# Contracting over all 128 rows: low key parts stored twice, compressed values zero-padded per head

## The chip, the cores and the metric

One core of one Trainium2 chip runs the kernel; the other cores are idle. The metric is the device time of one execution in microseconds (us), taken as the median of several runs.

## The reference, cut to what matters

Two decoder layers, sequence length 512, model width 1024, all in float32. Each layer normalises x, makes one wide projection, runs three token mixers on it (sparse attention, differential attention, a spatial gating MLP), merges them by gates, and ends with a SwiGLU FFN. The change touches the two attention mixers.

```python
# sparse attention (8 heads of 64 in 2 groups, query block of 128 rows)
logit_c = einsum('btghd,bngd->bghtn', qg, kc) * scale     # 31 compressed keys
p_c = masked_softmax(logit_c, ...)
o_cmp = einsum('bghtn,bngd->btghd', p_c, vc)              # compressed values
logit_s = einsum('btghd,bgtkd->bghtk', qrg, ks) * scale   # selected blocks, rotated keys
logit_w = einsum('btghd,bkgd->bghtk', qrg, kw) * scale    # window, rotated keys
out = g0 * o_cmp + g1 * o_slc + g2 * o_win
# differential attention (4 heads, two maps each, depth 64)
logits = einsum('bthd,bshd->bhts', q, k) * scale
a = p[:, :, 0] - lam * p[:, :, 1]
o = einsum('bhts,bshe->bthe', a, v)
```

Selected-block and window attention over 512 positions both come out as plain causal attention here, so the kernel has for each sparse head two causal maps ("kind" 0 and 1), and for each differential head two more.

## The kernel before, in words

To keep float32 accuracy with the fast float32r matmul, every operand is split into a high part (rounded) and a low part (the rest); a product takes three matmuls in the big GEMMs (high by high, low weight by high, high weight by low: lines 164 to 166). ScalarE makes the high part of each 128x1024 weight chunk (L144), VectorE or GpSimd the low part (L147), two chunks ahead of use; SyncE issues the weight loads (L125) four chunks ahead, with three raw buffers.

The work of a layer is a list of GEMM tasks. Two side lanes hold the attention work; after every GEMM step (three matmuls of 512 columns, counted as 650 ns) the side lanes are advanced by as many of their own steps as the count allows. So matmuls of attention lie between matmuls of GEMMs in TensorE's order, which is fixed when the program is built. Each `yield` in a lane is one such step.

Heads of depth 64 are stored so that rows 0 to 63 and 64 to 127 of a query tile hold the high and the low part. `rope_pair` rotates the four heads of a task, splits them, writes the parts to DRAM (L600) and reads them back in the layout wanted: the high part of the keys twice, on rows 0 to 63 and again on 64 to 127 (`kh`, L611); the low part of the keys once per head, two heads over each other in one tile `kl` (L614); the queries (`q2`) as high over low, or low over high for the heads that stand in the lower half of `kl` (L623, L626). `logits` (L778) then makes one block of 128 query rows in two matmuls: L783 over 128 rows gives (high + low) query by high key; L784 over 64 rows gives high query by low key. The block has 128, 256, 384 or 512 columns. `soft` subtracts the maximum (L773, VectorE) and takes the exponential (L775, ScalarE); `nsa` scales by sum and gate (L808 VectorE, L809 GpSimd), transposes by TensorE (L826), splits (L827 ScalarE, L833 VectorE) and multiplies by the values (L847); units follow each other at a distance of three (`LAG`). `diff` does the same with lines 917 to 949.

The compressed branch: `cmp_aux("v")` makes the compressed values of both groups, the same 32 rows four times over (`VCS`, L556 to L559: high in columns 0 to 63, low in 64 to 127). Its probabilities stand as `PcT`, 32 rows for each of four heads. For a head, L854 contracts over that head's 32 rows, twice (high and low part of the probabilities), into the accumulator `o` of L847.

Tiles come from pools: "t4" (36 buffers of 4 KB per row), "t2" (12 of 2 KB); logits have two PSUM banks ("s"), transposes two ("t"), accumulators one ("o"), GEMMs three ("g").

Of the kernel before, what the change touches and what calls it, by code (L numbers as in the profile page):

```python
# [11 lines left out]
F32 = mybir.dt.float32  # L12
# [15 lines left out]
# Emission distances: how many steps after its cause each part of a chain is traced.  # L28
D_FIN = (10, 17, 31, 34)        # norm of a differential head
D_CMP = (0, 5, 8, 12, 15, 26)   # softmax over compressed blocks  # L30
D_ROPE = (2, 11, 16, 19)        # split, store and reload of rotated heads
D_MX, D_ACT, D_OA, D_XP = (25, 27), (7, 19), (1, 4, 17), 2
D_NORM = (10, 13)              # must lie before the first evacuation of its group
W_NSA, W_DIFF, LAG = 500, 1300, 3
POOLED = {"w": 512, "u": 512, "g": 512}   # low-part columns made by GpSimd, by task
# [11 lines left out]
def chunk_table():  # L47
    """Name of each weight chunk of a layer -> (index, columns used)."""
# [27 lines left out]
class Kern:  # L76
# [12 lines left out]
    # ---------------------------------------------------------------- tiles  # L89
# [16 lines left out]
    # ----------------------------------------------------- delayed emission  # L106
# [13 lines left out]
    # -------------------------------------------------------------- weights  # L120
# [38 lines left out]
    # ----------------------------------------------------------- GEMM tasks  # L159
# [8 lines left out]
    def fm(self, i0, evacs, x, K=KT, late=False, hooks=None):  # L168
        """Feature-major products of len(evacs) weight chunks with the tiles x."""
# [20 lines left out]
    def tm(self, i0, x, evac, kper, n):  # L190
        """Token-major products: four token tiles, n columns."""
# [18 lines left out]
    # ------------------------------------------------------------- constants  # L210
# [44 lines left out]
    def pin(self, first, mark):  # L255
        """Instructions from first to mark stay in trace order on their engines, later ones behind them."""
# [18 lines left out]
    def setup2(self):  # L275
        """Differential lambda, halved merge bias, scaled sub-norm, rotary tables."""
# [99 lines left out]
    # ------------------------------------------------------------ RMS norms  # L376
    def make_xg(self, k, gcol, fast=None):
        """Gain-scaled high and low parts of x, and its squares."""
# [23 lines left out]
    def square0(self, k):  # L402
        """Squares of the first layer's input: two running sums, on two engines."""
# [40 lines left out]
    # --------------------------------------------------------- evacuations  # L444
# [66 lines left out]
    def cmp_aux(self, which):  # L511
# [32 lines left out]
        else:  # L544
# [15 lines left out]
            yield 1300  # L560

    def rope_pair(self, name, raw=None):
        """Evacuates the first- and second-half tiles of four heads, rotates and splits them."""
        st = {}

        def fa(ps):
# [930 lines left out]
```

## Time and profile before

| | us |
|---|---|
| median of 3 runs | 1886.5 |
| lowest, highest | 1885.8, 1887.4 |
| span of the profiled execution, first to last instruction | 1884.8 |
| TensorE busy in it | 1851.9 |
| VectorE busy in it | 1021.5 |
| ScalarE busy in it | 734.3 |
| GpSimd busy in it | 409.3 |

The three runs lie within 1.6 us. The span of the profiled execution is 1.7 us below the median. PE is TensorE's matmuls, PEld its weight loads, which may run beside matmuls; the end of a matmul in the trace is modelled, its start is not, so this text reads TensorE by the distance from one start to the next.

### The profile page before, as it was taken

To read this page: it belongs to the slowest core of one execution; us is meant where nothing else is said; L and a number is where in the kernel's file an instruction comes from. 1 tells how busy PE (TensorE), PEld (TensorE's weight loads), DVE (VectorE), ACT (ScalarE), POOL (GpSimd) and SP (SyncE) were. 2 spreads that over 40 slices of the span, in tenths; PEclk is the share of its full clock that TensorE was granted. 3 is DMA by queue.
4 is the path that set the end of the run, shared out by engine and by line. 5 is a ranking of instruction groups with operands and counts; after the bars stand their busy time and mean duration, and the time that the engine had idled before them with its cause. 6 is when DMAs were issued, how large, how long until landed. Compare 5 with 4: busy or idle time off the path is not lost.

```text
span 1884.8 us, 23458 instructions
## 1 busy us (share of the span) xinstructions
PE 1851.9 (98%) x8686; PEld 1493.7 (79%) x8686; DVE 1021.5 (54%) x1928; ACT 734.3 (39%) x1300; POOL 409.3 (22%) x391
## 2 busy tenths in 40 slices
PE   6999999999999999999999999999999999999997
PEld 5787777777888888888878877787778888888887
DVE  8657665557554444443355766656665544444323
ACT  4446554344333223222233555534443433223222
POOL 3324331234321000000042333313333200000001
PEclk9999999999999999999999999999999999999999
DMA  5542112543232222223346221154422322222221
GB/s 194 170 154 90 40 46 92 183 138 117 87 112 89 101 99 92 101 94 119 112 140 207 88 79 40 51 163 132 133 104 101 106 95 96 101 94 96 101 95 62
DMA packets 70787, 203.22 MB, mean 108 GB/s; under 512 B 9360, under 2 KB 11792, under 8 KB 70672
## 3 DMA queue, kind: packets, MB, share of 16 engines
q1 hardware_dynamic: 70672, 201.71, 32.1%
q8 instruction: 69, 1.13, 0.2%
q14 instruction: 46, 0.38, 0.1%
HBM read 182.67 MB, written 19.01 MB: 107 GB/s over the span
## 4 chain that ended last, share of the span: by engine, by line
PE 95%; DVE 2%; issue 2%; POOL 1%; DMA 0%; ACT 0%; DVEq 0%; SPq 0%; POOLq 0%
PE ps_g L164 26%; PE ps_g L165 25%; PE ps_g L166 25%; PE ps_s L784 3%; PE ps_o L847 2%; PE ps_t L826 2%; PE ps_s L783 2%; PE ps_g L203 1%; PE ps_g L202 1%; PE ps_g L201 1%; PE ps_o L945 1%; PE ps_o L854 1%; DVE wl L147 1%; POOL wl L147 1%; PE ps_o L203 0%
## 5 line engine op out<-in xcount | busy, mean ns | idle before, releaser
L164 PE MATMUL ps_g<-xg,wh 128*128 128x512 f32 x1408 | 573.6, 407 | 9.1 <-ACT wh L144 8.4
L144 ACT ACTIVATE wh<-wr 128x1024 fp32r<-128x1024 f32 (+2 forms) x324 | 318.2, 985 | 668.4 <-PE ps_g L166 369.2
L165 PE MATMUL ps_g<-xg,wl 128*128 128x512 f32 x1408 | 555.0, 394 | 7.0 <-DVE wl L147 7.0
L166 PE MATMUL ps_g<-xg,wh 128*128 128x512 f32 x1408 | 553.8, 393 | 0.0
L147 DVE TENSOR_TENSOR wl<-wr,wh 128x1024 fp32r<-128x1024 f32 (+2 forms) x312 | 358.1, 1149 | 227.2 <-ACT wh L144 226.0
L164 PEld LDWEIGHTS ps_g<-xg,wh 128*128 128x128 f32 x1408 | 266.7, 189 | 79.7 <-issue 12.5
L165 PEld LDWEIGHTS ps_g<-xg,wl 128*128 128x128 f32 x1408 | 266.9, 190 | 57.4 <-DVE wl L147 8.9
L166 PEld LDWEIGHTS ps_g<-xg,wh 128*128 128x128 f32 x1408 | 266.5, 189 | 56.4 <-issue 0.4
L775 ACT ACTIVATE e<-e,nm 128x128 f32<-128x128 f32 (+1 forms) x192 | 107.4, 559 | 137.3 <-DVE nm L773 134.3
L164 PE MATMUL ps_g<-act,wh 128*128 128x512 f32 (+1 forms) x374 | 141.0, 377 | 0.0
L165 PE MATMUL ps_g<-act,wl 128*128 128x512 f32 (+1 forms) x374 | 140.8, 376 | 0.0
L166 PE MATMUL ps_g<-act,wh 128*128 128x512 f32 (+1 forms) x374 | 140.8, 376 | 0.0
L147 POOL TENSOR_TENSOR wl<-wr,wh 128x512 fp32r<-128x512 f32 x72 | 112.2, 1563 | 83.0 <-ACT wh L144 77.6
L809 POOL TENSOR_SCALAR e<-e,sm,ga 128x128 f32<-128x128 f32 (+3 forms) x128 | 85.1, 666 | 180.3 <-DVE sm L808 167.4
L773 DVE CUSTOM_DVE_ANT_0 e<-ps_s,con 128x128 f32<-128x128 f32 (+1 forms) x192 | 93.1, 485 | 50.6 <-PE ps_s L784 48.9
L400 POOL TENSOR_TENSOR acc<-acc,sq 128x512 f32<-128x512 f32 x18 | 29.1, 1616 | 387.6 <-ACT sq L399 387.6
L1086 DVE TENSOR_TENSOR fb<-ps_g,R 128x512 f32<-128x512 f32 x44 | 30.4, 692 | 129.1 <-PE ps_g L166 129.1
L1077 DVE TENSOR_TENSOR fa<-ps_g,R 128x512 f32<-128x512 f32 x44 | 30.4, 692 | 95.6 <-PE ps_g L166 95.6
L166 PEld LDWEIGHTS ps_g<-act,wh 128*128 128x128 f32 x374 | 70.4, 188 | 13.0
L164 PEld LDWEIGHTS ps_g<-act,wh 128*128 128x128 f32 x374 | 70.4, 188 | 12.9
L165 PEld LDWEIGHTS ps_g<-act,wl 128*128 128x128 f32 x374 | 70.4, 188 | 12.8
L833 DVE TENSOR_TENSOR pt<-ps_t,pt 128x128 fp32r<-128x128 f32 (+3 forms) x128 | 61.9, 487 | 31.4 <-ACT pt L827 29.9
(229 smaller groups left out, 2589.0 us busy)
## 6 DMA issues: line engine op xcount, KB each, us to landing
wr<-in_wst SPq DMA_DIRECT2D x268, 512.0 KB, 3.2
rp_d<-pc SPq DMA_DIRECT2D x112, 128.0 KB, 2.6
wr<-in_wst SPq DMA_DIRECT2D x48, 256.0 KB, 2.7
kh<-rp_d SPq DMA_DIRECT2D x24, 256.0 KB, 4.3
xT<-in_xT SPq DMA_DIRECT2D x8, 512.0 KB, 5.6
q<-rp_d SPq DMA_DIRECT2D x16, 256.0 KB, 4.1
q<-rp_d SPq DMA_DIRECT2D x32, 128.0 KB, 3.5
kl<-rp_d SPq DMA_DIRECT2D x12, 256.0 KB, 6.2
```

Of the source, the lines that this page charges most:

```text
L144: nc.scalar.activation(h[:, a:b], t[:, a:b], AF.Copy)
L147: eng.tensor_tensor(lo[:, a:b], t[:, a:b], h[:, a:b].bitcast(F32), op=OP.subtract)
L164: nc.tensor.matmul(out, wh[:, c], xx[:, 0, ts], start=first, stop=False)
L165: nc.tensor.matmul(out, wl[:, c], xx[:, 0, ts], start=False, stop=False)
L166: nc.tensor.matmul(out, wh[:, c], xx[:, 1, ts], start=False, stop=last)
L773: nc.vector.tensor_tensor_reduce(out=e[:, :n], in0=s[:, :n], in1=self.mask[:, S - n:], scale=-0.125, scalar=3e38, op0=OP.add, op1=OP.min, ...
L775: nc.scalar.activation(e[:, :n], e[:, :n], AF.Exp, bias=nm, scale=-1.0, accum_out=sm)
L783: nc.tensor.matmul(s[:, :n], q[:, ts], k[:, :n], start=True, stop=False)
L784: nc.tensor.matmul(s[:, :n], q[r0:r0 + 64, ts], kl[r0:r0 + 64, :n], start=False, stop=True)
L809: nc.gpsimd.tensor_scalar(e[:, :n], e[:, :n], sm, gate, op0=OP.mult, op1=OP.mult)
L826: nc.tensor.transpose(pt[:, j, :], e[:, j * P:(j + 1) * P], self.ident)
L833: nc.vector.tensor_tensor(lo, pt, hi.bitcast(F32), op=OP.subtract)
```

## The change

The low parts of the keys are stored like the high parts: twice, on rows 0 to 63 and 64 to 127, in two tiles instead of one, loaded by four transfers instead of two. All query tiles are now high over low, one transfer of 128 rows per head. The second matmul of `logits` contracts over all 128 rows, (high + low) query by low key. The compressed values get a copy for each of the four heads, zero outside that head's 32 rows (four multiplications by columns of the block mask), and L854's matmul contracts over all 128 rows. `VCS` moves from a buffer of its own into the "t4" pool, and `cmp_aux("v")` has one more step. The other lines of the diff drop comments.

```diff
             for g in range(2):
                 for k in range(2):
                     nc.tensor.matmul(pv[:, g, :], hT[:, k, g].rearrange("p r n -> p (r n)"),
                                      w2[:, 512 + k * 64:512 + k * 64 + 64], start=(k == 0), stop=(k == 1))
-            self.VCS = self.const("VCS", [P, 2, P], F32R)
-            nc.scalar.activation(self.VCS[:, :, 0:64], pv, AF.Copy)
-            nc.vector.tensor_tensor(self.VCS[:, :, 64:128], pv, self.VCS[:, :, 0:64].bitcast(F32),
-                                    op=OP.subtract)
+            vcs = self.t2("vcs", (P, 2, P), F32R)
+            nc.scalar.activation(vcs[:, :, 0:64], pv, AF.Copy)
+            nc.vector.tensor_tensor(vcs[:, :, 64:128], pv, vcs[:, :, 0:64].bitcast(F32), op=OP.subtract)
             yield 1300
+            self.VCS = self.t4("VCS", [P, 4, 2, P], F32R)
+            for h in range(4):
+                col = C_BLK + 32 * h
+                nc.vector.tensor_scalar(self.VCS[:, h], vcs.bitcast(F32), self.con[:, col:col + 1], None,
+                                        op0=OP.mult)
+            yield 1300
...
                     kh = [self.t4("kh", [P, 2, S], F32R) for _ in range(2)]
-                    kl = self.t4("kl", [P, 2, S], F32R)
+                    kl = [self.t4("kl", [P, 2, S], F32R) for _ in range(2)]
                     for c in range(2):
-                        for r in range(2):
-                            nc.sync.dma_start(kh[c][64 * r:64 * r + 64].bitcast(F32),
-                                              d[0:64, 2 * c:2 * c + 2, :])
-                    for r in range(2):
-                        nc.sync.dma_start(kl[64 * r:64 * r + 64].bitcast(F32), d[64:128, r::2, :])
+                        for x, k in enumerate((kh, kl)):
+                            for r in range(2):
+                                nc.sync.dma_start(k[c][64 * r:64 * r + 64].bitcast(F32),
+                                                  d[64 * x:64 * x + 64, 2 * c:2 * c + 2, :])
                     self.rot[name] = (kh, kl)
                 else:
                     q = [self.t4("q2", [P, 2, S], F32R) for _ in range(2)]
                     for c in range(2):
                         for j in range(2):
                             h = 2 * c + j
-                            if (name == "QA1") or (name[1] == "B" and j == 1):
-                                for r in range(2):
-                                    nc.sync.dma_start(q[c][64 * r:64 * r + 64, j, :].bitcast(F32),
-                                                      d[64 - 64 * r:128 - 64 * r, h, :])
-                            else:
-                                nc.sync.dma_start(q[c][:, j, :].bitcast(F32), d[:, h, :])
+                            nc.sync.dma_start(q[c][:, j, :].bitcast(F32), d[:, h, :])
...
-    def logits(self, q, k, kl, r0, i):
+    def logits(self, q, k, kl, i):
+
         nc = self.nc
         n = (i + 1) * P
         ts = slice(i * P, (i + 1) * P)
         s = self.bank("s")
         nc.tensor.matmul(s[:, :n], q[:, ts], k[:, :n], start=True, stop=False)
-        nc.tensor.matmul(s[:, :n], q[r0:r0 + 64, ts], kl[r0:r0 + 64, :n], start=False, stop=True)
+        nc.tensor.matmul(s[:, :n], q[:, ts], kl[:, :n], start=False, stop=True)
         return s
...
-            s = self.logits(q2[hh // 2][:, hh % 2], kh[kind][:, g], kl[:, kind], 64 * g, i)
+            s = self.logits(q2[hh // 2][:, hh % 2], kh[kind][:, g], kl[kind][:, g], i)
...
-                rows = slice(32 * hh, 32 * hh + 32)
                 for x in range(2):
-                    nc.tensor.matmul(o, self.VCS[rows, g, :],
-                                     self.PcT[g][rows, x, half * 256:half * 256 + 256],
+                    nc.tensor.matmul(o, self.VCS[:, hh, g, :],
+                                     self.PcT[g][:, x, half * 256:half * 256 + 256],
                                      start=False, stop=(x == 1))
...
-            s = self.logits(q2[c][:, j], kh[c][:, j], kl[:, c], 64 * j, i)
+            s = self.logits(q2[c][:, j], kh[c][:, j], kl[c][:, j], i)
```

## Rows read from the trace of the kernel before

**Rows 1.** The page: the span, busy time of TensorE and VectorE (share of the span, instructions), and the chain of work that ended last, by engine.

```profile
span 1884.8 us, 23458 instructions
PE 1851.9 (98%) x8686; PEld 1493.7 (79%) x8686; DVE 1021.5 (54%) x1928; ACT 734.3 (39%) x1300; POOL 409.3 (22%) x391
...
PE 95%; DVE 2%; issue 2%; POOL 1%; DMA 0%; ACT 0%; DVEq 0%; SPq 0%; POOLq 0%
```

**Rows 2.** Busy time of each engine in stretches of the span (start:end in us, length, then busy us and instructions of each engine, granted TensorE clock, busy share of the DMA engines, GB/s): two stretches of the first layer's sparse attention, one of its differential attention, and the first stretch of the second layer's sparse attention.

```profile
130.00:165.00 35.00, 35.00 (x184) 26.50 (x183) 30.85 (x103) 25.15 (x76) 18.36 (x25) 1.00 0.21 64
165.00:200.00 35.00, 34.99 (x179) 25.82 (x178) 22.24 (x67) 19.44 (x51) 12.17 (x17) 1.00 0.23 73
370.00:410.00 40.00, 40.00 (x187) 30.83 (x187) 24.24 (x64) 16.95 (x38) 13.93 (x12) 1.00 0.63 170
1055.00:1090.00 35.00, 35.00 (x181) 26.42 (x181) 31.08 (x104) 25.01 (x77) 18.65 (x24) 1.00 0.20 65
```

**Rows 3.** Groups of TensorE instructions with their shapes kept apart: rows x columns of the weights and of the streamed operand, how many, busy us, mean ns of one. L784 comes in four widths, 48 of each; the widest and the narrowest are shown.

```profile
L784 PE MATMUL ps_s<-kl,q 64*128 64x512 f32 x48 | 23.8, 496 | 0.0
...
L854 PE MATMUL ps_o<-pcT,VCS 32*128 32x256 f32 x64 | 15.9, 327 | 0.0
L784 PE MATMUL ps_s<-kl,q 64*128 64x128 f32 x48 | 15.5, 324 | 0.0
```

**Rows 4.** The weight loads of L784 in the same view: count, busy us, mean ns, then the idle time of the weight loader just before them and what it was put down to.

```profile
L784 PEld LDWEIGHTS ps_s<-kl,q 64*128 64x128 f32 x192 | 35.1, 183 | 49.0 <-issue 47.0
```

**Rows 5.** TensorE's instructions in order of time around one logits block of 512 columns (start us, duration us): first the matmuls, then three of the weight loads.

```profile
230.87 0.40 PE L783 MATMUL ps_s<-kh,q 128*128 128x512 f32 x1
231.20 0.50 PE L784 MATMUL ps_s<-kl,q 64*128 64x512 f32 x1
231.63 0.50 PE L164 MATMUL ps_g<-xg,wh 128*128 128x512 f32 x1
231.96 0.39 PE L165 MATMUL ps_g<-xg,wl 128*128 128x512 f32 x1
232.19 0.40 PE L166 MATMUL ps_g<-xg,wh 128*128 128x512 f32 x1
...
231.20 0.18 PEld L784 LDWEIGHTS ps_s<-kl,q 64*128 64x128 f32 x1 [0.37 <-issue]
231.62 0.19 PEld L164 LDWEIGHTS ps_g<-xg,wh 128*128 128x128 f32 x1 [0.25 <-issue]
231.73 0.19 PEld L165 LDWEIGHTS ps_g<-xg,wl 128*128 128x128 f32 x1
```

**Rows 6.** The same for one block of 128 columns.

```profile
175.00 0.22 PE L783 MATMUL ps_s<-kh,q 128*128 128x128 f32 x1
175.15 0.32 PE L784 MATMUL ps_s<-kl,q 64*128 64x128 f32 x1
175.40 0.50 PE L164 MATMUL ps_g<-xg,wh 128*128 128x512 f32 x1
175.74 0.39 PE L165 MATMUL ps_g<-xg,wl 128*128 128x512 f32 x1
```

**Rows 7.** The same around one pair of compressed-value products (x2, x4: instructions merged into one row).

```profile
171.50 0.60 PE L826 MATMUL ps_t<-con,e 128*128 128x128 f32 x4
171.85 0.65 PE L847 MATMUL ps_o<-pt,v 128*128 128x256 f32 x4
172.44 0.50 PE L854 MATMUL ps_o<-pcT,VCS 32*128 32x256 f32 x2
172.87 0.50 PE L164 MATMUL ps_g<-xg,wh 128*128 128x512 f32 x1
173.21 0.40 PE L165 MATMUL ps_g<-xg,wl 128*128 128x512 f32 x1
```

**Rows 8.** The first stretch of the sparse attention, columns as in rows 2 for TensorE and its weight loads, counting L784 alone, then L854 alone.

```profile
130.00:165.00 35.00, 5.63 (x14) 2.56 (x14) 1.00 0.21 64
...
130.00:165.00 35.00, 0.99 (x4) 0.58 (x4) 1.00 0.21 64
```

**Rows 9.** One unit of the sparse attention in order of time: its low logits product, the first and the last step of its softmax, and the copy of its transposed weights.

```profile
193.96 0.38 PE L784 MATMUL ps_s<-kl,q 64*128 64x256 f32 x1
194.48 0.42 DVE L773 CUSTOM_DVE_ANT_0 e<-ps_s,con 128x256 f32<-128x256 f32 x1 [0.58 <-PE ps_s L784]
...
195.85 0.56 POOL L809 TENSOR_SCALAR e<-e,sm,ga 128x256 f32<-128x256 f32 x1 [1.98 <-DVE sm L808]
...
201.85 0.39 ACT L827 ACTIVATE pt<-ps_t 128x256 fp32r<-128x256 f32 x1 [0.28 <-PE ps_t L826]
```

**Rows 10.** Waits of the weight loader from 128 to 300 us: total us, times, longest us.

```profile
PEld ps_t L826 <- POOL e L809: 0.6, 3, 0.2
```

**Rows 11.** VectorE in order of time behind the making of VCS in the first layer, and two products of the same form as the four that are added (512 columns each).

```profile
77.99 2.36 DVE L147 TENSOR_TENSOR wl<-wr,wh 128x1024 fp32r<-128x1024 f32 x2 [0.65 <-ACT wh L144]
83.85 0.69 DVE L581 TENSOR_TENSOR t<-ps_g,sinR 128x512 f32<-128x512 f32 x1 [3.49 <-PE ps_g L166]
...
119.28 0.88 DVE L667 TENSOR_SCALAR v<-v,rv 128x512 f32<-128x512 f32 x2 [1.16 <-POOL rv L662]
```

**Rows 12.** DMA issues on SyncE's queue: count, KB each, median us from issue to landing.

```profile
q<-rp_d SPq DMA_DIRECT2D x32, 128.0 KB, 3.5
kl<-rp_d SPq DMA_DIRECT2D x12, 256.0 KB, 6.2
```

## The prediction, made before the changed kernel was run

> **What bounds the kernel now.** I read the page first. TensorE is busy for 98% of the span and holds 95% of the chain that ended last, so time is won or lost on TensorE [rows 1]. The second view is busy time by stretches. In the attention stretches TensorE is at 35.0 us of 35, its clock at 1.00, the upper of its two levels (2.4 GHz), and no other engine is near full but one: VectorE has 30.85 us of work in the first 35 us of the sparse attention, 31.08 in the second layer's, and 22.24 in the stretch behind it [rows 2].
>
> "Busy" hides something, because the ends of matmuls are modelled. So the third view is TensorE in order of time, read by the distance from start to start. A 128-row matmul of 512 columns costs 0.23 us in a dense run (231.96 to 232.19). The 64-row matmul of a logits block does not fit in: from L783 to L784 it takes 0.33, from L784 to the next matmul 0.43, and that one needs 0.33 [rows 5]. Three slots of 512 columns take 231.96 - 230.87 = 1.09 us where dense ones take 0.69: 0.40 us more. The weight loads say where it goes: L165's load lies inside L164's matmul, but L784's load begins 0.37 us after its predecessor's load ended, with L783 almost through, and the next 128-row load waits again, 0.25 us [rows 5]. Over the kernel the loader idles 49.0 us in front of L784's 192 loads, 47.0 of them put down to no engine at all [rows 4].
>
> **Part 1: the low logits product over 128 rows (192 matmuls, four widths, 48 of each [rows 3]).** At 512 columns the surplus is 0.40 us. At 128 columns three slots take 175.74 - 175.00 = 0.74 us [rows 6]; dense ones would take 0.23 + 2 x 0.09, the 0.09 from four transposes of 128 columns in 0.35 us [rows 7], together 0.41, so the surplus is 0.33. The two widths between lie between. I take 0.37: 192 x 0.37 = 71 us; bounds 192 x 0.33 = 63 and 192 x 0.40 = 77.
>
> The number of matmuls and of streamed columns stays; rows cost nothing by themselves, since L783 with 128 rows and L784 with 64 stream the same columns. What must hold is that a matmul with 128-row weights behind another such has its load hidden. L165 behind L164 shows it [rows 5].
>
> The Trainium skill has a rule against this change: "TensorE: Matmul & The Clock Gate", Part 3, says that a weight load overlaps with matmuls in flight only when its row group differs. By it a 128-row load would be exposed behind every 128-row matmul, and the sum here would be nothing or a loss. The trace disagrees: L165's load (231.73 to 231.92) runs within L164's matmul, of the same rows [rows 5]. Another page, "TensorEngine Tiling (Array Packing)", Tiling Modes, says that changing the tiling mode drains the array; the two waits around L784 are what that would look like, and by it the whole surplus goes.
>
> **Part 2: compressed values over 128 rows (64 matmuls, in 32 pairs [rows 3]).** From the L847 group to the second matmul behind a pair it takes 173.21 - 171.85 = 1.36 us [rows 7]. Dense, six slots of 256 columns (half of 0.23 each) and one of 512 make 0.92. Surplus 0.44 per pair, 32 x 0.44 = 14 us; should the four L847 themselves be slower than half a wide slot, 0.40, which is 13.
>
> Gross gain: 71 + 14 = 85 us, bounds 76 and 91.
>
> **Part 3: what is added.** Four VectorE products of 128x256 per layer. A product of that form with 512 columns took 0.88 / 2 = 0.44 us [rows 11], so four cost at most 1.8 us and at least half that. They come one step after VCS, behind the 2.36 us of low-part work that ends at 80.35; VectorE then idles 3.49 us until 83.85, waiting for TensorE [rows 11]. That idle time hides them: 0. Should they get ahead of the low parts, these are 1.8 us late, and they are made two chunks ahead: still 0 in the middle case, 2 us per layer at worst.
>
> Key loads grow by two transfers of 256 KB for each of six key tasks, which queue ahead of weight chunks on SyncE; query loads shrink, from 32 halves of 128 KB to 16 whole ones [rows 12]. The differential stretch has the DMA engines 63% busy, the sparse ones about 20% [rows 2]. A transfer takes 6.2 us to land [rows 12], and the two more go beside the others; chunks are asked for four ahead. I take 0, at most 6 x 0.5 us = 3.
>
> The extra low-key tile and VCS take two more of the 36 "t4" buffers. Counted off the program's order, at most 29 are alive at once in the sparse attention before, 31 after: 0.
>
> **Part 4: what is late next.** With the surplus gone the same VectorE work must fit in less time. The first stretch holds 14 L784 and 4 L854 [rows 8]: 14 x 0.37 + 2 x 0.44 = 6 us, so TensorE would need 29 us where VectorE works 30.85 [rows 2]. VectorE becomes the bound there: 2 us per layer if it never idled, 4 if half of its present 4.15 us of idling stays. I take 3 per layer, 6 in all; bounds 4 and 8. Elsewhere VectorE has 22.24 us [rows 2] for 28 to 29: it fits. The softmax chain of a unit ends 196.41 - 193.96 = 2.45 us after its logits, and its transposes are copied only at +7.89 [rows 9]; a fifth less time leaves some 6, so the distance of three units still covers it. TensorE now waits there three times, 0.6 us in all [rows 10]. I take 2 us, from 0.
>
> **Sum.** 85 - 6 - 2 = 77 us. The span 1884.8 becomes 1807.8; the median lies 1.7 us above the span now, so 1809.5, rounded to 1809.
>
> **Rivals.**
> - *VectorE and the softmax latency become the bound in all attention stretches.* For: 30.85 of 35 already, and in-order queues wait before they are full. Against: rows 9 and 10. If each of the 192 logits blocks waited 0.15 us more, 29 us would come back: about 1838. Chance 0.12.
> - *The rows are not the cause.* The surplus would belong to accumulating twice into one logits bank, or to the change from high to low operands, and stay. For: L784 always follows L783 into the same bank. Against: L854, with 32 rows, has the same surplus, and L847 and the GEMMs accumulate into one bank without it [rows 5, 7]. Then only the additions count: 1886 to 1889. Chance 0.03.
> - *Key loads block SyncE's queue (slower).* A low-key tile that found no free "t4" buffer would hold its loads, and behind them every weight chunk. Chunks four ahead, 24 matmuls of 0.23 us each, are 22 us of cover; the six key tasks would each have to be held for 22 + 85 / 6 = 36 us before the time is above the old one; at 40 us it would be 1910. Against: the count of 31 in 36. Chance 0.03.
> - *More is gained.* All 91 us, and nothing is given back: 1886.5 - 91 = 1795.5. Chance 0.07.
>
> The forecast, with its small losses, has 0.75, and its own range is 1800 to 1822.
>
> **The range.** The forecast's 0.75 and the nearer half of the first rival make about 0.8: 1800 to 1834. A difference under 0.2% (4 us) can't be told from none here. Faster: forecast, first and last case, 0.94. Same: 0.03, from the second rival. Slower: 0.03.
>
> **What would show it.** Right: L784 as 128*128, start to start 0.23 at 512 columns on both sides; no idle time put down to "issue" in front of its loads; L854 at half that; the four products in VectorE's gap near 80 us; the FFN stretches as long as before; the attention of each layer shorter by some 38 us; TensorE waiting for VectorE or GpSimd, if anywhere, in the first 35 us of the sparse attention. Wrong: surplus slots around L784 still there; or dense slots, but gaps in front of L783 (no free logits bank) or L826 (softmax not done); or ScalarE's chunk split waiting for DMA behind key loads.

## The result, and the profile after

The changed kernel takes 1820.1 us (median of 4 runs, 1818.8 to 1827.1) against 1886.8 us before (4 runs, 1885.8 to 1887.4): a ratio of 0.9655, 95% interval 0.9638 to 0.9673 (of the means, which the run of 1827.1 us pulls up; the medians give 0.9647). By the medians that is 66.7 us less. The forecast was 1809 us, 77.5 less than the 1886.5 us shown with the profile before, and its range 1800 to 1834 holds the time. 11 us of the forecast gain did not come.

The page after, first the span, then busy times, then the chain of work that ended last, by engine (before: [rows 1]):

```profile
span 1818.7 us, 23473 instructions
PE 1778.1 (98%) x8686; PEld 1489.3 (82%) x8686; DVE 1017.8 (56%) x1936; ACT 731.9 (40%) x1300; POOL 411.6 (23%) x391
...
PE 90%; DVE 3%; issue 3%; POOL 2%; ACT 1%; DMA 1%; DVEq 0%; POOLq 0%; SPq 0%; ACTq 0%
```

TensorE still sets the end, but its share of the chain fell from 95 to 90%: something besides TensorE now counts. What became of the surplus slots is in the groups by shape (before: [rows 3, 4]) and in TensorE's order of time (before: [rows 5 to 7]):

```profile
L784 PE MATMUL ps_s<-kl,q 128*128 128x512 f32 x48 | 18.8, 391 | 0.0
L853 PE MATMUL ps_o<-pcT,VCS 128*128 128x256 f32 x64 | 14.5, 308 | 0.0
L784 PE MATMUL ps_s<-kl,q 128*128 128x128 f32 x48 | 13.1, 273 | 0.0
L784 PEld LDWEIGHTS ps_s<-kl,q 128*128 128x128 f32 x192 | 36.2, 188 | 6.0
```

```profile
222.45 0.40 PE L783 MATMUL ps_s<-kh,q 128*128 128x512 f32 x1
222.68 0.40 PE L784 MATMUL ps_s<-kl,q 128*128 128x512 f32 x1
222.92 0.27 PE L826 MATMUL ps_t<-con,e 128*128 128x128 f32 x1
...
226.60 0.66 PE L847 MATMUL ps_o<-pt,v 128*128 128x256 f32 x4
227.09 0.45 PE L853 MATMUL ps_o<-pcT,VCS 128*128 128x256 f32 x2
227.38 0.29 PE L783 MATMUL ps_s<-kh,q 128*128 128x256 f32 x1
```

A block of 512 columns runs at dense slots, 0.23 and 0.24 us from start to start, where it took 0.33 and 0.43 [rows 5]. The loader idles 6.0 us before L784's loads instead of 49.0 [rows 4], and none of it is "issue" any more. The compressed-value pair (L853 now, L854 before) takes 0.29 us instead of 0.43 [rows 7], the four L847 ahead of it 0.49 instead of 0.59. So the mechanism is the predicted one. The waits of the weight loader show what came in its place (total us, times, longest us). First before, then after; before's L757 and L974 are L756 and L973 after, the same transposes.

```profile
PEld ps_s L784 <- issue: 47.0, 170, 0.4
PEld ps_g L164 <- issue: 15.4, 69, 0.9
PEld ps_g L164 <- ACT wh L144: 8.6, 2, 7.1
PEld ps_t L974 <- issue: 3.4, 4, 1.4
PEld ps_t L826 <- issue: 2.5, 12, 0.2
PEld ps_t L826 <- POOL e L809: 1.2, 6, 0.2
PEld ps_o L847 <- ACT pt L827: 0.9, 4, 0.2
PEld ps_t L757 <- issue: 0.7, 2, 0.4
```

```profile
PEld ps_g L164 <- ACT wh L144: 13.1, 4, 7.2
PEld ps_s L783 <- DVE nm L772: 5.2, 12, 0.9
PEld ps_t L756 <- issue: 3.0, 2, 1.5
PEld ps_t L826 <- POOL e L809: 2.9, 6, 0.9
PEld ps_t L973 <- issue: 2.9, 2, 1.5
PEld ps_o L847 <- ACT pt L827: 2.4, 8, 0.5
PEld ps_t L826 <- issue: 0.8, 2, 0.4
```

The first two lines of before (62.4 us) are gone but for 0.9 us of L164 behind "issue". The other six of before make 17.3 us, the seven of after 30.3, so 13 us are new, nearly all of it waits for other engines (10.7 before, 23.6 after). Lines of the view that are not shown fell by some 3 us.

To see where the time went, take the start of the same GEMM matmul (lines 164 to 166, and 201 to 203, their like with tokens as rows; numbered from 0) in two traces: before minus another kernel is what that kernel has gained by then. The table gives the gain by stage, us, with the kernels of the experiments below. It uses the 300th (before at 108.1 us), 900th (337.1), 1500th (512.8), 3600th (1008.2), 4200th (1237.2) and 5100th matmul (1481.0).

| kernel | start-up | sparse, layer 1 | differential, layer 1 | FFN and start of layer 2 | sparse, layer 2 | differential, layer 2 |
|---|---|---|---|---|---|---|
| after | 0.7 | 23.6 | 7.7 | 0.6 | 23.6 | 9.3 |
| e6 both narrow | 0.8 | -0.3 | -1.7 | 0.6 | -0.2 | -3.3 |
| e1 logits narrow | 0.4 | 5.0 | -3.3 | 0.8 | 5.0 | -3.2 |
| e2 values narrow | -1.5 | 18.6 | 7.9 | 1.2 | 18.6 | 7.8 |
| e4 64 rows twice | 0.5 | -6.6 | -8.2 | 1.5 | -6.5 | -8.3 |
| e3 96 rows | -2.7 | 23.4 | 9.2 | 0.9 | 23.5 | 9.2 |
| e7 queries in halves | 0.7 | 23.3 | 9.9 | 2.3 | 23.4 | 9.8 |
| e8 no low weights | 0.1 | 23.3 | 7.8 | -0.8 | 23.4 | 7.7 |
| e9 copy later | 0.3 | 23.6 | 9.8 | 1.5 | 23.7 | 9.7 |
| e10 distance 4 | -2.0 | 22.8 | 7.7 | 0.9 | 22.9 | 9.3 |
| e11 600 ns | -0.8 | 19.5 | 7.7 | -1.5 | 19.8 | 7.8 |
| e12 transposes later | 2.3 | 22.1 | 8.0 | -1.0 | 22.1 | 9.3 |
| e13 halves, copy later | -0.8 | 23.4 | 10.7 | -1.4 | 23.4 | 10.7 |

Behind the 5100th matmul no kernel changes by more than 0.1 us. Start-up scatters by 2 to 3 us between kernels of the same instruction order (e2 and e3 against after), and the fifth column by as much over all. The sparse attention agrees to 0.3 us between the two layers of a kernel, the differential one to 1.6.

The differences of 1.6 go with TensorE's granted clock. In the two rows below (columns as in [rows 2]), each around the same wait of TensorE in the differential attention, it is 0.91 in after's first layer and 1.00 in its second. In the first, TensorE has waited 2.04 us up to 384.78 for ScalarE; from 386.31 to 386.73 a matmul of 512 columns then takes 0.42 us, the pace of the lower of the clock's two levels (1.2 GHz). In the second it has waited as long, and the clock stays at the upper one (2.4 GHz).

```profile
380.00:400.00 20.00, 17.91 (x86) 14.97 (x85) 11.86 (x26) 7.40 (x13) 9.23 (x7) 0.91 0.22 79
1272.00:1292.00 20.00, 17.91 (x93) 15.04 (x92) 12.79 (x28) 7.39 (x13) 9.29 (x7) 1.00 0.24 80
```

Taken over the whole stage, the granted clock is 0.99 in the first layer's differential attention of after, e1, e2, e4, e8, e10, e11 and e12, and in the second layer's of e6, e1, e2, e4, e8 and e11; in all other differential stages, before's too, it is 1.00. Where a kernel has the same clock in both layers, the two gains agree to 0.1 us; where it hasn't, the layer at 0.99 gains 1.3 to 1.6 less. Start-up goes the same way: before has 0.94 there, e3 with the largest loss 0.92, e12 with the largest gain 0.98; but e2 and e10 lose 1.5 and 2.0 us at after's 0.95, so the clock isn't all of it. So a few us of a median are no evidence by themselves; a stage's gain in both layers, at the same clock, is.

### The profile page after: what moved, and what is told of

Its sections match the earlier page's. It is cut to its first block, busy times and chain, and to the rows that moved or that the text cites. A ratio compares the mean times of both kernels' runs of the same rounds, so it can differ in the third digit from the quotient of the medians.

```text
span 1818.7 us, 23473 instructions
## 1 busy us (share of the span) xinstructions
PE 1778.1 (98%) x8686; PEld 1489.3 (82%) x8686; DVE 1017.8 (56%) x1936; ACT 731.9 (40%) x1300; POOL 411.6 (23%) x391
## 4 chain that ended last, share of the span: by engine, by line
PE 90%; DVE 3%; issue 3%; POOL 2%; ACT 1%; DMA 1%; DVEq 0%; POOLq 0%; SPq 0%; ACTq 0%
PE ps_g L164 25%; PE ps_g L165 25%; PE ps_g L166 25%; PE ps_o L847 2%; PE ps_t L826 2%; PE ps_g L202 1%; PE ps_g L201 1%; PE ps_s L784 1%; PE ps_g L203 1%; PE ps_s L783 1%; POOL wl L147 1%; PE ps_o L944 1%; DVE wl L147 1%; PE ps_o L203 0%; PE ps_o L201 0%
## 5 line engine op out<-in xcount | busy, mean ns | idle before, releaser
L144 ACT ACTIVATE wh<-wr 128x1024 fp32r<-128x1024 f32 (+2 forms) x324 | 318.7, 987 | 664.7 <-PE ps_g L166 368.5
L164 PE MATMUL ps_g<-xg,wh 128*128 128x512 f32 x1408 | 561.7, 399 | 13.3 <-ACT wh L144 12.6
L166 PE MATMUL ps_g<-xg,wh 128*128 128x512 f32 x1408 | 553.6, 393 | 0.0
L147 DVE TENSOR_TENSOR wl<-wr,wh 128x1024 fp32r<-128x1024 f32 (+2 forms) x312 | 363.9, 1168 | 226.0 <-ACT wh L144 225.2
L164 PEld LDWEIGHTS ps_g<-xg,wh 128*128 128x128 f32 x1408 | 267.0, 190 | 65.7 <-ACT wh L144 13.1
L164 PE MATMUL ps_g<-act,wh 128*128 128x512 f32 (+1 forms) x374 | 141.0, 377 | 0.0
L400 POOL TENSOR_TENSOR acc<-acc,sq 128x512 f32<-128x512 f32 x18 | 29.1, 1615 | 387.6 <-ACT sq L399 387.6
L772 DVE CUSTOM_DVE_ANT_0 e<-ps_s,con 128x128 f32<-128x128 f32 (+1 forms) x192 | 91.6, 481 | 18.1 <-PE ps_s L784 17.4
L164 PEld LDWEIGHTS ps_g<-act,wh 128*128 128x128 f32 x374 | 70.4, 188 | 12.9
L1128 POOL TENSOR_TENSOR acc<-acc,sq 128x512 f32<-128x512 f32 x5 | 6.9, 1381 | 316.6 <-ACT sq L1126 316.6
```

Of the source, the lines that this page charges most:

```text
L144: nc.scalar.activation(h[:, a:b], t[:, a:b], AF.Copy)
L147: eng.tensor_tensor(lo[:, a:b], t[:, a:b], h[:, a:b].bitcast(F32), op=OP.subtract)
L164: nc.tensor.matmul(out, wh[:, c], xx[:, 0, ts], start=first, stop=False)
L166: nc.tensor.matmul(out, wh[:, c], xx[:, 1, ts], start=False, stop=last)
L772: nc.vector.tensor_tensor_reduce(out=e[:, :n], in0=s[:, :n], in1=self.mask[:, S - n:], scale=-0.125, scalar=3e38, op0=OP.add, op1=OP.min, ...
```

## Experiments: are the rows the cause?

Five kernels keep the order, storage and transfers of after and change only how many rows a product contracts over: the low logits product in e1, e3, e4 and e6, the compressed values in e2 and e6. Rows 64 to 127 of the query tile are its low part, so e1 and e6 compute what before computes; e3 takes half of the low by low product, e4 adds the low keys' product a second time.

**e1: the low logits product back on 64 rows.**

```diff
-        nc.tensor.matmul(s[:, :n], q[:, ts], kl[:, :n], start=False, stop=True)
+        nc.tensor.matmul(s[:, :n], q[0:64, ts], kl[0:64, :n], start=False, stop=True)
```

> The changed kernel with one thing undone: L784 contracts over rows 0 to 63 of the same tiles (high query by low key, as before). Storage, transfers and the order of all instructions are those of the changed kernel. Theory (the row count of L784 is the cause): 0.33 to 0.40 us per block come back, 192 times, less what tighter stretches give away, so 60 to 71 us more than the changed kernel, 1880 to 1891 us; start to start around a 512-column L784 again 0.33 and 0.43 us. Rival (accumulating twice into one bank, or the layout of the parts, is the cause): 1820 us as the changed kernel.

Measured: 1881.0 us, ratio to before 0.9969 (0.9956 to 0.9982), 60.9 over after. TensorE in order of time:

```profile
228.14 0.40 PE L783 MATMUL ps_s<-kh,q 128*128 128x512 f32 x1
228.47 0.50 PE L784 MATMUL ps_s<-kl,q 64*128 64x512 f32 x1
228.90 0.50 PE L164 MATMUL ps_g<-xg,wh 128*128 128x512 f32 x1
229.24 0.40 PE L165 MATMUL ps_g<-xg,wl 128*128 128x512 f32 x1
```

The slots of before are back, 0.33, 0.43 and 0.34 us, to the hundredth but one [rows 5]. Nothing but the rows of this one matmul differs from after, so the rows cost at least 61 us.

**e2: the compressed values back on 32 rows.**

```diff
-                    nc.tensor.matmul(o, self.VCS[:, hh, g, :],
-                                     self.PcT[g][:, x, half * 256:half * 256 + 256],
+                    nc.tensor.matmul(o, self.VCS[32 * hh:32 * hh + 32, hh, g, :],
+                                     self.PcT[g][32 * hh:32 * hh + 32, x, half * 256:half * 256 + 256],
```

> The changed kernel with L853 (L854 before) contracting over the head's 32 rows of the new VCS tile; all else, the order too, as in the changed kernel. Theory: 32 pairs at 0.40 to 0.44 us, 13 to 14 us more than the changed kernel, 1830 to 1834 us; as little as 8 more where a pair stands beside a wait. Rival (rows are not the cause): 1820 us.

Measured: 1833.9 us, ratio 0.9717 (0.9703 to 0.9732), 13.8 over after. By the table 2.2 of it arose at start-up, ahead of any attention, and 1.5 in the second layer's differential attention, where e2 has the lower clock and after hasn't; the sparse attention lost 5.0 per layer. With the waits for ScalarE that went away beside the slower pairs, the 32 pairs cost some 10 to 11 us, not 14.

**e6: both narrow.** The edits of e1 and e2 together; what is left of the change is storage, transfers and order.

> The changed kernel with L784 over 64 rows and L853 over 32: the old matmuls, but the new storage, transfers, VCS products and instruction order. If those four cost nothing at the old pace, 1886 to 1888 us, as before, and the 11 us that the gain falls short of come from the tighter stretches alone. If the new order or the transfers cost the 11 us by themselves, 1895 to 1898 us.

Measured: 1890.8 us (10 runs), ratio 1.0023 (1.0013 to 1.0033): 4.0 us over before, 70.7 over after. So the rows alone bring 70.7, and all the rest of the change costs 4 (2.5 to 6.2 by the interval). The table puts that loss in the differential attention, none in the sparse: 1.7 in the first layer, at a clock of 1.00, and 3.3 in the second, at 0.99. So about 1.7 per layer is the new order, storage and transfers themselves; the other 1.6 is the clock, which in e6's second layer fell behind TensorE's wait for L144 that ends at 1340.60. In the waits of e6 one line differs from before by more than a microsecond:

```profile
PEld ps_g L164 <- ACT wh L144: 12.8, 4, 7.1
```

It was 8.6 in two places. After has it too (13.1, 4). What stands behind it is in ScalarE's queue, here that of after in the first layer's differential attention, with TensorE's wait under it:

```profile
382.60 0.60 ACT L953 ACTIVATE do<-ps_o 128x512 f32<-128x512 f32 x1 [1.34 <-PE ps_o L944]
383.10 0.68 ACT L975 ACTIVATE ob<-ps_t,sub 128x512 fp32r<-128x512 f32 x1
383.67 2.53 ACT L144 ACTIVATE wh<-wr 128x1024 fp32r<-128x1024 f32 x3
...
384.78 0.50 PE L164 MATMUL ps_g<-xg,wh 128*128 128x512 f32 x1 [2.04 <-ACT wh L144]
```

In after's program the copy L953 stands ahead of the three weight splits L144; before, the first of them stood ahead of it. It waits for its own product (1.34 us of idle time), the splits wait behind it, and TensorE waits 2.04 us for them. The order of the instructions is made when the program is built, from the tiles and transfers it is given; with those of the change it came out otherwise. Which of them moved the copy was not tried; e7 below, with two tasks' query loads in halves again, still has the copy ahead.

**e3: 96 rows.**

```diff
-        nc.tensor.matmul(s[:, :n], q[:, ts], kl[:, :n], start=False, stop=True)
+        nc.tensor.matmul(s[:, :n], q[0:96, ts], kl[0:96, :n], start=False, stop=True)
```

> The changed kernel with L784 over 96 rows (it leaves out the low query by low key products of the last 32 rows); all else as in the changed kernel, the order too. Theory (the array has a few row modes, and the cost is the change of mode; 96 rows are run in the mode of 128): 1820 us, no surplus around L784. Rival 1 (any count under 128 pays the full surplus): 1881 us, as with 64 rows. Rival 2 (the cost grows with the rows left idle): half of it, 1850 us.

Measured: 1823.0 us, ratio 0.9664 (0.9648 to 0.968). In the sparse attention it is after within 0.2 us; its 3.4 us at start-up lie ahead of any logits, at a granted clock of 0.92 against after's 0.95.

```profile
225.96 0.40 PE L783 MATMUL ps_s<-kh,q 128*128 128x512 f32 x1
226.19 0.40 PE L784 MATMUL ps_s<-kl,q 96*128 96x512 f32 x1
226.42 0.27 PE L826 MATMUL ps_t<-con,e 128*128 128x128 f32 x1
```

Slots of 0.23 on both sides: 96 rows beside 128 cost nothing, 64 beside 128 cost 0.4 us. So it isn't that the row counts differ, and the cost doesn't grow evenly with the idle rows.

**e4: the 64-row product twice.**

```diff
-        nc.tensor.matmul(s[:, :n], q[:, ts], kl[:, :n], start=False, stop=True)
+        for x in range(2):
+            nc.tensor.matmul(s[:, :n], q[0:64, ts], kl[0:64, :n], start=False, stop=x == 1)
```

> The kernel of e1 with the 64-row L784 issued twice behind L783, so that the low product is added twice: a second narrow matmul next to the first. Theory (the surplus is paid for changing from 128 rows to 64 and back, not for a narrow matmul as such): each second one costs a plain slot, 48 x (0.23 + 0.17 + 0.12 + 0.10) = 30 us over e1, 1911 us. Rival (each narrow matmul pays): 30 + 61 us over e1, 1972 us.

Measured: 1915.3 us, ratio 1.0151 (1.0136 to 1.0166), 34.3 over e1. The second narrow matmul costs 34.3 / 192 = 0.18 us on average over the four widths. Dense slots in after are 0.23 us at 512 columns, 0.17 at 384, 0.12 at 256 and 0.11 at 128, 0.16 in the mean, so the second narrow matmul costs hardly more than its slot. Had it a surplus of its own like the first, 0.3 us more would stand on each of the 192. So the surplus is paid per change between 128 and 64 rows and back, 0.3 to 0.4 us for both changes, and not per narrow matmul.

The second rival (the rows are not the cause) falls with e1 and e6.

## Experiments: what took 11 us of the forecast?

**e9: the copy L953 two steps later** (the wait found with e6).

```diff
-            nc.scalar.activation(o, OB.pop(c), AF.Copy)
+            ob = OB.pop(c)
+            self.later(2, lambda: nc.scalar.activation(o, ob, AF.Copy), "ob")
```

> The changed kernel with ScalarE's copy of a differential head's accumulator (L953) emitted two steps later, so that in ScalarE's queue it stands behind the weight splits L144 that it stood ahead of. Theory (TensorE's wait of 2.0 us in each layer for L144 comes from that queue order): 4 to 5 us less than the changed kernel, 1815 to 1816 us, and the wait gone. Rival (the split would be late anyway, for a buffer or its load): 1819 to 1821 us, the wait still there.

Measured: 1818.7 us, ratio 0.9636 (0.9622 to 0.9651), 1.4 under after, which the medians alone don't tell from none. The differential attention gained 9.8 and 9.7 instead of 7.7 and 9.3. The waits:

```profile
PEld ps_g L164 <- ACT wh L144: 10.8, 4, 7.7
PEld ps_o L944 <- ACT do L954: 2.0, 2, 1.0
```

Much of it moved: 2.3 us less for the splits, 2.0 us new, where the next product must wait until its bank is copied out. 2.1 and 0.4 us were won in the stage, of which 1.6 is the clock: it fell in after's first layer and not in e9's. At the same clock the later copy is worth some 0.4 us per layer. The expected 4 to 5 us were too many, and the wait was in the main moved, not removed.

**e7: the query loads in halves.** The whole change, but two tasks load their second heads in two halves of 64 rows as before, now high over low. This leaves TensorE's order in the sparse attention as it was before; in after some units stand elsewhere.

```diff
-                            nc.sync.dma_start(q[c][:, j, :].bitcast(F32), d[:, h, :])
+                            if (name == "QA1") or (name[1] == "B" and j == 1):
+                                for r in range(2):
+                                    nc.sync.dma_start(q[c][64 * r:64 * r + 64, j, :].bitcast(F32),
+                                                      d[64 * r:64 * r + 64, h, :])
+                            else:
+                                nc.sync.dma_start(q[c][:, j, :].bitcast(F32), d[:, h, :])
```

> The whole change, but the queries that were loaded in two halves of 64 rows before still come in two halves (high over low now). With it the program's order in the sparse attention is that of the kernel before; the copies L953 that stand ahead of weight splits in the differential attention stay ahead. Theory (the new order costs 1.9 and 3.5 us where it differs in the differential attention, as e6 against the kernel before shows, and nothing in the sparse one): 1819 to 1821 us. Rival (the new order in the sparse attention costs part of the missing gain): 1812 to 1816 us.

Measured: 1819.9 us, ratio 0.9644 (0.9629 to 0.9658). The sparse attention gains 23.3 and 23.4, after 23.6: the new order there cost nothing, and the rival falls.

**e8: VectorE without the low part of the attention weights.** L833 is left out and L847's product with the low part takes a tile of zeros, so TensorE's work stays and the result lacks that part.

```diff
-            lo, pt, hi = LO.pop(u)
-            nc.vector.tensor_tensor(lo, pt, hi.bitcast(F32), op=OP.subtract)
+            LO.pop(u)
```

> The changed kernel without VectorE's 128 low parts of the sparse weights (L833, 62 us of VectorE work); L847 multiplies by a tile of zeros in their place, so TensorE's work is the same, and the low parts are left out of the result. Theory (what the tighter stretches give back is VectorE's doing: logits banks and transposes' banks come free late): 10 to 14 of the 15 us given back return, 1806 to 1810 us, and TensorE's waits on L772 and L808 go. Rival (the softmax chain's length or the order of the queues): 1816 to 1821 us.

Measured: 1822.9 us, ratio 0.9663 (0.9649 to 0.9677); no gain at all, and above what either theory allowed; 1.6 us of that is the lower clock in the second layer's differential attention. VectorE's load did fall, from 33.50 us (after) to 29.09 in the same 35 us:

```profile
130.00:165.00 35.00, 33.57 (x200) 28.50 (x199) 33.50 (x112) 26.87 (x81) 19.79 (x26) 1.00 0.27 80
```

```profile
130.00:165.00 35.00, 33.79 (x200) 28.35 (x199) 29.09 (x100) 27.18 (x82) 19.96 (x25) 1.00 0.26 76
```

The waits for VectorE stayed all the same: L783 behind L772 is 5.2 us in 12 places in both. Of the softmax chain's waits, L847's 2.4 us behind ScalarE went, and L826 waits 2.3 us more in their place (3.1 instead of 0.8, put down to no engine). The reason can be read at the longest wait for L772. First a product of the gating MLP (L671) of after, then VectorE, and under it the matmul that waits:

```profile
136.10 1.06 PE L671 MATMUL ps_s<-sw,v 128*128 128x128 f32 x8
...
136.79 1.76 DVE L691 TENSOR_TENSOR oc<-stmp,oc 128x128 fp32r<-128x128 f32 x4
138.46 1.21 DVE L147 TENSOR_TENSOR wl<-wr,wh 128x1024 fp32r<-128x1024 f32 x1
...
139.67 0.66 DVE L737 TENSOR_REDUCE cmx<-ce 128x16 f32<-128x512 f32 x1
...
140.33 0.27 DVE L772 CUSTOM_DVE_ANT_0 e<-ps_s,con 128x128 f32<-128x128 f32 x1
...
141.57 1.12 DVE L678 SCALAR_TENSOR_TENSOR stmp<-ps_s,par,sw 128x128 f32<-128x128 f32 x4
...
140.66 0.39 PE L783 MATMUL ps_s<-kh,q 128*128 128x256 f32 x1 [0.49 <-DVE nm L772]
```

The block of 128 columns whose bank L772 must free was multiplied at 137.29; VectorE takes it up only at 140.33, because four splits of the gating MLP (L691), a whole weight chunk and a step of the compressed softmax stand ahead of it, without a pause between them. No L833 is among them. The other of the two logits banks is no help here: the gating MLP takes its products from the same two (`bank("s")` in line 669), and the one that L671 filled at 136.10 is read by L678 only from 141.57. So at this place each logits block must wait for the one just before it. In e8 the same instructions stand there and TensorE waits the same 0.49 us. So it isn't the amount of VectorE's work in the stretch that sets the wait, but what stands in its queue directly ahead of L772 at that place, while the other bank is taken. This is read from the trace; a kernel with that order changed, or with a bank of its own for the gating MLP, wasn't tried.

**e10 to e12: more distance.** Three single numbers, one each: units of the sparse attention four steps apart instead of three; its steps counted as 600 ns instead of 500; the transposes L756 of the compressed branch four steps later.

```diff
-W_NSA, W_DIFF, LAG = 500, 1300, 3
+W_NSA, W_DIFF, LAG = 500, 1300, 4
```

> The units of the sparse attention follow each other at a distance of four instead of three, nothing else. Theory (what the changed kernel gives back in the sparse attention is the latency of a unit's softmax chain): the waits of L826 for GpSimd's weights (2.9 us, 6) and of L847 for ScalarE's copy (2.4 us, 8) go, the gain over before behind each sparse attention grows from 24 to 26 or 27 us, and the time is 1814 to 1817 us. Rival (those waits are the visible end of VectorE's or the logits banks' delay, which would end the same instruction a little later): the waits change their name, the time is 1818 to 1822.

```diff
-W_NSA, W_DIFF, LAG = 500, 1300, 3
+W_NSA, W_DIFF, LAG = 600, 1300, 3
```

> The sparse attention's steps are counted as 600 ns instead of 500, so that more GEMM matmuls lie between two logits blocks; nothing else. Theory (the logits banks: L783 waits for VectorE's minimum of the block two before, 5.2 us in 12 places, since the blocks lie too close in time for a chain of fixed length): these waits go, 1813 to 1816 us, or less where the stretch of the softmax chain gains too. Rival (the waits are at a few places where VectorE's queue holds something else first, and density does not matter): 1818 to 1822. Should the longer side lane run past the GEMMs that cover it, the time is over 1823 and the end of a layer's attention shows it.

```diff
-D_CMP = (0, 5, 8, 12, 15, 26)
+D_CMP = (0, 5, 8, 12, 19, 26)
```

> The transposes of the compressed branch (L756) come four steps later behind the softmax over compressed blocks (15 becomes 19), nothing else. Theory: their wait (3.0 us in 2 places, one per layer) is the latency of that chain and goes: 1816 to 1818 us. Rival: the wait moves to the next instruction of the chain, 1819 to 1821.

Measured: e10 1824.7 us (ratio 0.9669, 0.9653 to 0.9685), e11 1832.9 (0.9708, 0.9693 to 0.9722), e12 1825.5 (0.9672, 0.9658 to 0.9687). All three missed their theory, and e10 and e12 lie above their rival's range too. For e11 the third case named beforehand came: the last compressed-value product of the first layer (L853) starts at 291.9 us instead of 282.6, and 4.2 of the 5.2 us of waits for L772 are still there. In the sparse attention the gains in the first layer are 22.8, 19.5 and 22.1 against 23.6, so distance does not help, and a longer side lane costs. e12 shows how such a wait moves:

```profile
PEld ps_t L826 <- POOL e L809: 9.2, 12, 1.3
PEld ps_t L756 <- issue: 1.8, 2, 0.9
```

L756 waits 1.8 instead of 3.0 us, and L826, behind it in TensorE's queue, waits 9.2 for GpSimd instead of 2.9.

**e13: halves and late copy together** (e7 and e9), to see whether a version beats after.

> The whole change, with two edits together: the query loads of two tasks stay in halves of 64 rows (which leaves TensorE's order in the sparse attention as it was before) and ScalarE's copy in the differential attention comes two steps later (so that weight splits are not behind it). Theory (the wait for weight splits behind that copy is worth up to 3 us, the order in the sparse attention nothing): 1816 to 1818 us, some 2 to 4 us under the changed kernel; L164's wait for ScalarE falls from 13.1 to about 10 us. Rival (the wait only moves to the instruction that reads the copy): 1819 to 1821.

Measured: 1819.8 us, ratio 0.9638 (0.9625 to 0.9652). The differential attention gains 10.7 in both layers, the most of all kernels and 1.4 over after's layer at the same clock, and L164 waits 9.9 us for ScalarE. So e13's two edits win back most of the 1.7 us per layer that e6 lost there. But start-up and the start of layer 2 took back 2.2, both at a lower clock than after's (0.94 against 0.95, and 0.99 against 1.00). By their medians three versions lie within 1.5 us of after, and none is shown to beat it.

## Why the prediction was right, and where its sum was off

The mechanism and the sign were right, the time 11 us too low. The gross gain was taken some 6 to 8 us too high, and a cost of 4 us was not in the sum; both errors went the same way, so the time does not lie in the range because errors cancelled. By steps:

- **The surplus is per logits block and goes with 128 rows: right.** e1 and the slots show it. The size 71 was near: e1 is 60.9 us slower than after, and in it the waits that after has gained are gone again (L826, L756 and L783 as in e6), some 8 us that hid in the surplus. That makes about 69, an estimate.
- **Compressed values 14 us: over-sized.** One pair was measured, 0.44; e2 gives 10 to 11 over 32 pairs, 0.33 each. The pair read was a slow one: the four L847 ahead of it took 0.59 us from first start to the pair's, 0.51 in the median.
- **Gross 85: 77 to 79.** e6 minus after is 70.7; after waits 30.3 us by the names listed above, e6 21.9 by the same names, so 8.4 us of the gross were given back: 70.7 + 8.4 = 79. By all lines of the view, in the four attention stages alone, it is 6.8, and the gross 77.5. Inside the bounds 76 and 91, but 6 to 8 below the value taken. This is the larger mis-sized term.
- **Given back 8: right in size (7 to 8), in part in place, wrong in its reason.** The prediction had 3 of it per layer in the first 35 us of the sparse attention, because VectorE had 30.85 us of work there. From 130 to 165 us of e6, after gains 3.5 us by the start of the same GEMM matmuls where the prediction's gross was 6, so some 2.5 were given back there. The rest lies in the later sparse and the differential attention, for which the prediction had 2 in all. But e8 shows that less VectorE work in that stretch wins nothing: VectorE is not the bound. That the size came out is luck; a share of busy time did not price it, the queue in front of L772 and the bank held by the gating MLP do.
- **TensorE's order fixed, and storage free: the step that failed.** The sum had nothing for the order of other engines. It changed with the change's tiles and transfers, the copy L953 came ahead of the weight splits, and e6 prices order, storage and transfers together at 4.0 us (2.5 to 6.2). By the table that is 1.7 per layer of differential attention, and 1.6 where the clock fell behind the longer wait; the prediction read the clock as 1.00 and had no term for that either. e13, which reorders ScalarE in two places, wins 1.4 of the 1.7 back, and L164's wait for ScalarE falls from 13.1 to 9.9 us; which part of the change made the rest was not tried. This is the term that was not in the sum. 70.7 - 4.0 = 66.7 adds up because both numbers come from e6, so this is a ledger, not a proof.
- **The four VectorE products come behind the low-part work: wrong, at no price.** Three stand ahead of it, at 76.43; VectorE still idles 3.27 us until 83.11 (before 3.49 until 83.85), and start-up is no later than before (0.7 us earlier, at a clock of 0.95 against 0.94).

```profile
76.43 0.88 DVE L563 TENSOR_SCALAR VCS<-vcs,con 128x256 fp32r<-128x256 f32 x3
77.22 1.22 DVE L147 TENSOR_TENSOR wl<-wr,wh 128x1024 fp32r<-128x1024 f32 x1
...
83.11 0.69 DVE L586 TENSOR_TENSOR t<-ps_g,sinR 128x512 f32<-128x512 f32 x1 [3.27 <-PE ps_g L166]
```

- **Key loads free: right for the end, though weight chunks do come later.** ScalarE's waits for the raw chunk (before, then after) are the sign of "wrong" that the prediction named:

```profile
ACT wh L144 <- DMA wr<-in_wst: 8.7, 5, 3.7
```

```profile
ACT wh L144 <- DMA wr<-in_wst: 37.4, 13, 6.5
```

  The two longest, 6.53 us at 317.75 and 6.35 at 1210.22, lie between the stages of attention; e6 has 34.8 us of it, so it comes with the transfers and not with the rows. TensorE's own waits for L144 are not at those places: of the 13.1 us, 7.2 are at the start and 1.5 at 942.06, both as before, and 2.18 at 384.78 and at 1277.43 stand behind the copy shown with e6. The chunks are late within their lead. Whatever it costs is inside e6's 4 us, and the rival with SyncE's queue blocked for 36 us and more did not come.
- **FFN as long as before: right**; **38 us per layer's attention: 31 and 33.** Of the 7 missing in the first layer, 4 are in the differential attention (11.8 expected, 32 blocks of 0.37; 7.7 came), of which 1.6 is the clock and 1.7 the order; 3 are in the sparse.
- **The rival of VectorE and the softmax bounding all stretches (1838)** did not come; what came of it is the 7 to 8 us given back.

The rule weighed in the prediction, of the Trainium skill, "TensorE: Matmul & The Clock Gate", Part 3 (a weight load overlaps only when its row group differs), taken as the prediction took it, would have made the change worth nothing; the same part also lets a load into a background weight buffer be pulled ahead, and the trace fits that: here 128-row loads behind 128-row matmuls run hidden, 0.23 us from start to start, and the change is worth 66.7 us. The other, "TensorEngine Tiling (Array Packing)", Tiling Modes (a change of tiling mode drains the array, another tile of the same mode does not), has modes of 128, 64 and 32 rows only, and e3 and e4 agree with it: 96 rows at no surplus, a second 64-row matmul at 0.18 us. That 96 rows run in the mode of 128 is an inference; no run shows the mode itself.

## What to carry to other kernels

A matmul that contracts over 64 rows, or a pair over 32, between matmuls of 128 rows costs its slots and some 0.3 to 0.4 us for the two changes; pad with zeros or stored copies, or put the narrow ones side by side. Read it by start-to-start distances and the loader's idle time, since busy shares show nothing (98% before and after). When a bound engine gets faster, price what is late next by the queue directly ahead of each awaited instruction, not by the busy share of the stretch, ask which other products hold the same banks, and put down a few us for the order that comes out anew when tiles or transfers change. Before a stage's gain of a microsecond or two is explained, compare the granted clock of that stage in both traces.

## What the runs showed of the hardware that was not expected

- 96 rows beside 128 rows stream and load like 128: 0.23 us per 512 columns, no wait (e3). 64 rows have the surplus; no count between 64 and 96 was run.
- A second narrow matmul in a row has no surplus: 34.3 us over 192 (e4).
- A change to 32 rows and back around a pair cost 0.33 us (e2), a change to 64 and back about as much (69 / 192 = 0.36).
- The same wait of 2.04 us was followed by a fall of the granted clock in after's first layer (0.91 over 20 us) and by none in its second (1.00); the fall cost the stage 1.6 us. No run shows what decides it.
